# Row maxima of a 16,384 x 1,024 matrix: other blocks and loads, four half-row pieces at the end, and a written order of VectorE's steps

## The chip, the core and the metric

The kernel runs on one core of a Trainium2 chip. The metric is the time of one execution on the device in microseconds (us); lower is better. The profile is one such execution, seen by the hardware profiler.

## What is computed

```python
def setup_inputs():
    batch, seq, dim = 32, 512, 1024
    return {"x": np.random.randn(batch, seq, dim).astype(np.float32)}

def reference(x):
    return np.max(x, axis=-1).astype(np.float32)
```

The input is 16,384 rows of 1,024 float32 numbers, 67.1 MB. The output is the largest number of each row, 64 KB. Each number is read once and compared once, so the kernel is a stream of loads with a reduction behind it.

## The kernel before

**Layout.** The rows are cut into two blocks, of 112 and 16 + 2 = 18 rows for each of the 128 partitions. In a block, a partition owns consecutive rows of the input, so a load of n rows brings n x 4,096 consecutive bytes to each partition. `BLOCKS` lists the rows of the 17 loads; the last two rows of each partition come in three pieces. The loads land in `ring`, an SBUF buffer of 46 rows a partition, and the results gather in `res`, one column for each of a partition's 128 rows.

**VectorE** reduces each load to one number a row with `reduce_max` along the row (the helper `maximum`, L168). Each such reduction of load j is called here the direct reduction, `d`j.

**TensorE, ScalarE and GpSimd** take over a part. `SHARED` says of five loads how many of their last rows (m) are shared, and how many of the eight 128-column parts of such a row (parts) do not go to VectorE. A 128 x 128 part is called a block of a shared row; there are 38. For them `turn` (L125) transposes up to eight blocks with TensorE into PSUM (`ps`), ScalarE copies them to SBUF (`sb`), and GpSimd takes the maximum over the partitions with one `partition_all_reduce` (`top`, L143). `back` (L154) moves the results, one row of 128 numbers a block, back across the partitions with TensorE, into a small PSUM tile of the load (`fetched`, handed out by `share`). VectorE writes the maximum of the columns that it kept into a further column of the same tile (the partial reduction, `p`j), and `merge` (L170) reduces the tile's columns into `res` (`m`j). `MERGE` says after which load's steps a merge stands.

**Order.** Every computing engine works in the order in which the program emits its instructions (`in_turn` chains them). The loop over the loads emits VectorE's steps in the order of the loads, and TensorE's by the list `TENSOR`. Loads are issued on SyncE's queue, up to three ahead in the program's order, each as soon as the steps that still read its place in the ring are emitted; on the chip an issue then waits for these steps to be done.

**The end.** The row before last and the last row come as pieces of 689, 671 and 688 elements: the second holds the end of one row and the start of the next, and VectorE reduces both halves of it in one instruction (`res<-res 128x2`). The results of the first part of a row are put beside the elements that follow, so that the next reduction takes them in. Three stores of the first block's results, issued by ScalarE, wait for the first piece's reduction (`latest_row`), so that they run behind the loads; the second block's results are stored last.

Of the kernel before, what the change touches and what calls it, by code (L numbers as in the profile page):

```python
# [8 lines left out]
F32 = mybir.dt.float32  # L9
# [1 line left out]


BLOCKS = [
    [15, 15, 15, 14, 12, 11, 9, 8, 7, 6],
    [4, 3, 2, 2, 1, 1, 1],
]
RING = 46


SHARED = {7: (2, 3), 9: (4, 4), 11: (3, 3), 13: (2, 3), 16: (1, 1)}  # L20


TENSOR = [
    ("turn", 7, 0), ("back", 7, 0), ("turn", 9, 0), ("turn", 9, 1),
    ("back", 9, 0), ("turn", 11, 0), ("turn", 11, 1), ("back", 9, 1),
    ("turn", 13, 0), ("back", 11, 0), ("back", 11, 1), ("turn", 16, 0),
    ("back", 13, 0), ("back", 16, 0),
]

MERGE = {8: (7,), 12: (9,), 15: (11,), 18: (13, 16)}  # L30
NOSYNC = mybir.DependencyInfo(mybir.DependencyClass.NoSync, mybir.DependencyReason.DATA)
SYNC = mybir.DependencyInfo(mybir.DependencyClass.Sync, mybir.DependencyReason.DATA)


@with_exitstack
def kernel(
    ctx: ExitStack,
    tc: tile.TileContext,
    x: bass.AP,
    out: bass.AP,  # L40
):
    nc = tc.nc
    P = 128
    X = mybir.AxisListType.X
    ALU = mybir.AluOpType

    xf = x.flatten_outer_dims()
    N, D = xf.shape
    H = D // 2
    C = D // P  # L50
    I = N // P
    of = out.flatten_outer_dims()

    once = ctx.enter_context(tc.tile_pool(name="once", bufs=1))
    turned = ctx.enter_context(tc.tile_pool(name="turned", bufs=2))
    allr = ctx.enter_context(tc.tile_pool(name="allr", bufs=2))
    psum = ctx.enter_context(tc.tile_pool(name="psum", bufs=2, space=bass.MemoryType.PSUM))
    psmall = ctx.enter_context(tc.tile_pool(name="psmall", bufs=4, space=bass.MemoryType.PSUM))
    ring = once.tile([P, RING, D], F32)

    W = 336
    K = W - 1
    AT = I + 16
    MID = AT + K + W + 17
    res = once.tile([P, MID + D - W], F32)

    latest = {}

    def in_turn(engine, inst):

        if engine in latest:
            tc.add_manual_dep(inst.ins, latest[engine].ins.name, NOSYNC, reason="in turn")
        latest[engine] = inst
        return inst

    ident = once.tile([P, P], F32)  # L80
    colno = once.tile([P, P], F32)
    rowno = once.tile([P, 32], F32)
    in_turn("DVE", nc.vector.memset(ident, 1.0))  # L83
    in_turn("DVE", nc.vector.memset(rowno, 0.0))  # L84
    in_turn("DVE", nc.vector.tensor_tensor_scan(  # L85
        out=colno, data0=ident, data1=ident, initial=-1.0, op0=ALU.add, op1=ALU.mult))
    in_turn("DVE", nc.vector.transpose(out=rowno, in_=colno[:, :32]))  # L87
    for q in range(1, P // 32):
        part = rowno[q * 32:(q + 1) * 32, 0:1]
        in_turn("DVE", nc.vector.tensor_scalar(  # L90
            out=part, in0=part, scalar1=float(q * 32), scalar2=None, op0=ALU.add))
    in_turn("DVE", nc.vector.tensor_scalar(  # L92
        out=ident, in0=colno, scalar1=rowno[:, 0:1], scalar2=None, op0=ALU.is_equal))

    loads = []
    first = at = 0
    views = []
    for sizes in BLOCKS:
        S = sum(sizes) + 2 * (sizes is BLOCKS[-1])
        xb = xf[first * P:(first + S) * P, :].rearrange("(p i) d -> p i d", p=P)  # L100
        dst = bass.AP(tensor=of.tensor, offset=of.offset + first * P, ap=[[S, P], [1, S]])
        views.append((dst, res[:, first:first + S]))
        b = 0
        for n in sizes:
            if at + n > RING:
                at = 0
            loads.append((at, n, xb[:, b:b + n, :], first + b))
            at += n
            b += n
        first += S  # L110
    assert first == I

    def chunks(j):
        m, parts = SHARED[j]
        per = max(1, C // parts)
        return [(r, min(per, m - r)) for r in range(0, m, per)]

    def rows(j):
        start, n, _, _ = loads[j]
        return ring[:, start:start + n, :]  # L120

    tops = {}
    backs = {}

    def turn(j, c):  # L125


        m, parts = SHARED[j]
        r, q = chunks(j)[c]
        W = q * parts * P  # L130
        ps = psum.tile([P, D], F32)
        for i in range(q):
            for c0 in range(parts):
                k = i * parts + c0
                in_turn("PE", nc.tensor.transpose(  # L135
                    out=ps[:, k * P:(k + 1) * P],
                    in_=rows(j)[:, loads[j][1] - m + r + i, c0 * P:(c0 + 1) * P],
                    identity=ident,
                ))
        sb = turned.tile([P, D], F32)  # L140
        in_turn("ACT", nc.scalar.copy(out=sb[:, :W], in_=ps[:, :W]))  # L141
        top = allr.tile([P, D], F32)
        in_turn("POOL", nc.gpsimd.partition_all_reduce(  # L143
            top[:, :W], sb[:, :W], P, bass_isa.ReduceOp.max))
        tops[j, c] = top

    def share(j):
        m, parts = SHARED[j]
        if j not in backs:
            fetched = psmall.tile([P, parts + (parts < C), m], F32)  # L150
            backs[j] = fetched
        return backs[j]

    def back(j, c):  # L154

        m, parts = SHARED[j]
        r, q = chunks(j)[c]
        for i in range(q):
            for c0 in range(parts):
                k = i * parts + c0  # L160
                in_turn("PE", nc.tensor.transpose(  # L161
                    out=share(j)[:, c0, r + i:r + i + 1],
                    in_=tops[j, c][0:1, k * P:(k + 1) * P],
                    identity=ident[0:1, 0:1],
                ))

    def maximum(out, in_):
        return in_turn("DVE", nc.vector.reduce_max(out=out, in_=in_, axis=X))  # L168

    def merge(j):  # L170
        for i in MERGE.get(j, ()):
            _, k, _, c0 = loads[i]
            q, _ = SHARED[i]
            maximum(res[:, c0 + k - q:c0 + k], share(i).rearrange("p k m -> p m k"))


    issued = done = 0
    todo = list(TENSOR)
    for j in range(len(loads)):
        while issued < len(loads) and issued < j + 3:  # L180
            start, n, src, _ = loads[issued]
            held = any(s < start + n and start < s + k for s, k, _, _ in loads[j:issued])
            if held:
                break
            nc.sync.dma_start(out=rows(issued), in_=src)
            issued += 1
        while todo and todo[0][1] < (j if todo[0][0] == "back" else issued):
            what, i, c = todo.pop(0)
            (turn if what == "turn" else back)(i, c)
        _, n, _, col = loads[j]  # L190
        m, parts = SHARED.get(j, (0, 0))
        if n > m:
            maximum(res[:, col:col + n - m], rows(j)[:, :n - m, :])
        if m and parts < C:
            maximum(share(j)[:, parts, :], rows(j)[:, n - m:, parts * P:])
        merge(j)
    for what, i, c in todo:
        assert what == "back"
        back(i, c)

    if at + 1 > RING:
        at = 0
    piece = ring[:, at, :D - K]
    nc.sync.dma_start(out=piece, in_=xb[:, S - 2, :D - K])
    pair = xb[:, S - 2:, :].rearrange("p i d -> p (i d)")
    nc.sync.dma_start(out=res[:, AT:AT + K + W], in_=pair[:, D - K:D + W])
    nc.sync.dma_start(out=res[:, MID:], in_=pair[:, D + W:])
    latest_row = maximum(res[:, AT - 1:AT], piece)
    merge(len(loads))


    maximum(
        bass.AP(tensor=res.tensor, offset=res.offset + I - 2,
                ap=[list(res.ap[0]), [MID - 1 - (I - 2), 2]]),
        res[:, AT - 1:AT + K + W].rearrange("p (r k) -> p r k", r=2))
    merge(len(loads) + 1)
    maximum(res[:, I - 1:I], res[:, MID - 1:])


    for p, q in ((0, 48), (48, 96), (96, P)):  # L220
        store = nc.scalar.dma_start(out=views[0][0][p:q], in_=views[0][1][p:q])
        tc.add_manual_dep(store.ins, latest_row.ins.name, SYNC, reason="behind the loads")
    nc.scalar.dma_start(out=views[1][0], in_=views[1][1])


# [1 line left out]
_INS = ['x']  # L227
# [26 lines left out]
```

## Time and profile before

| | |
|---|---|
| time, median of 3 runs | 164.12 us (164.04 to 164.16) |
| span in the profile | 162.3 us |
| VectorE busy | 135.4 us |
| TensorE, ScalarE, GpSimd busy | 14.0, 6.3, 16.2 us |
| loads | 67.11 MB on queue q1 |

In the profile, DVE is VectorE, PE is TensorE's matrix multiplication, PEld its load of weights, ACT is ScalarE and POOL is GpSimd. A digit of a slice is the busy share of one fortieth of the span, in tenths. In a row of a group stand the line and engine, what is written from what, the shapes, then the busy time and the mean of one instruction, and after the second bar how long the engine was idle before it and what ended that. In a timeline, a row begins with the start and the duration in us; a bracket gives the idle time before it. A transpose of TensorE shows as MATMUL.

### The profile page before, as it was taken

Reading aid. Unit: us, or ns where it says so; the run is one execution under the profiler, and the core shown is the slowest. Engines: PE = TensorE matmul, PEld = TensorE weight load, DVE = VectorE, ACT = ScalarE, POOL = GpSimd, SP = SyncE. Lnnn points to the kernel's source line nnn. Section 1 sums busy time; section 2 is a strip of 40 time slices with the busy share of each in tenths; the row PEclk is TensorE's granted clock in tenths of the full one; section 3 lists DMA queues with packets and bytes.
Section 4 is the critical chain, followed back from the end, with each engine's and each line's share of the span. In section 5 each row is a group of like instructions: output and inputs, shape, how many; then the busy total and the mean of one; then the engine's idle time right before and its main releaser. Section 6 shows DMA issues by size and latency. Waiting matters only on the chain.

```text
span 162.3 us, 305 instructions
## 1 busy us (share of the span) xinstructions
PE 14.0 (9%) x76; PEld 12.0 (7%) x76; DVE 135.4 (83%) x35; ACT 6.3 (4%) x8; POOL 16.2 (10%) x11
## 2 busy tenths in 40 slices
PE   0000000000000000000000000000003010736540
PEld 0000000000000000000000000000002010725440
DVE  3000079995999779998999999999999999999994
ACT  3000000000000000000000000000001000222020
POOL 0000000000000000000000000000000500095970
DMA  7999699988999699999998998999999999999990
GB/s 242 485 485 454 273 485 485 485 379 348 485 485 485 285 410 452 452 452 388 497 472 371 433 455 355 436 436 420 509 396 445 452 395 396 440 411 423 405 379 18
DMA packets 3200, 67.18 MB, mean 414 GB/s; under 512 B 640, under 2 KB 640, under 8 KB 1408
## 3 DMA queue, kind: packets, MB, share of 16 engines
q1 hardware_dynamic: 2880, 67.11, 96.7%
q10 hardware_dynamic: 320, 0.07, 0.2%
HBM read 67.11 MB, written 0.07 MB: 414 GB/s over the span
## 4 chain that ended last, share of the span: by engine, by line
DVE 57%; DMA 36%; issue 5%; DVEq 0%
DVE res L168 52%; DMA ring<-in_x_dram 36%; DVE fetched L168 5%; DVEq L249 0%
## 5 line engine op out<-in xcount | busy, mean ns | idle before, releaser
L168 DVE TENSOR_REDUCE res<-ring 128x15 f32<-128x15360 f32 (+10 forms) x15 | 124.1, 8302 | 23.7 <-DMA ring<-in_x_dram 23.7
L143 POOL PARTITION_ALL_REDUCE top<-sb x7 | 16.0, 2330 | 141.8 <-ACT sb L141 141.8
L135 PE MATMUL ps<-ident,ring 128*128 128x128 f32 x38 | 9.3, 425 | 133.8 <-DMA ring<-in_x_dram 133.8
L135 PEld LDWEIGHTS ps<-ident,ring 128*128 128x128 f32 x38 | 7.5, 223 | 134.1 <-issue 127.8
L141 ACT COPY sb<-ps 128x768 f32<-128x768 f32 (+3 forms) x7 | 5.1, 739 | 150.2 <-PE ps L135 150.2
L168 DVE TENSOR_REDUCE fetched<-ring 128x2 f32<-128x1280 f32 (+3 forms) x5 | 8.5, 1699 | 0.0
L161 PE MATMUL fetched<-ident,top 1*128 1x1 f32 x38 | 4.8, 243 | 10.8 <-DVE fetched L168 7.3
L161 PEld LDWEIGHTS fetched<-ident,top 1*128 1x128 f32 x38 | 4.5, 213 | 12.5 <-issue 8.0
L168 DVE TENSOR_REDUCE res<-res 128x2 f32<-128x672 f32 (+1 forms) x2 | 1.7, 858 | 0.0
L141 ACT ACT_TABLE_LOAD x1 | 1.3, 1283 | 0.7 <-PEq L238 0.7
L83 DVE MEMSET ident<- 128x128 f32 x1 | 0.2, 165 | 0.8 <-PEq L238 0.8
L168 DVE TENSOR_REDUCE res<-fetched 128x2 f32<-128x8 f32 (+3 forms) x5 | 0.7, 158 | 0.0
L90 DVE TENSOR_SCALAR rowno<-rowno 32x1 f32<-32x1 f32 x3 | 0.4, 146 | 0.1
L85 DVE TENSOR_TENSOR_SCAN colno<-ident 128x128 f32<-128x128 f32 x1 | 0.4, 425 | 0.0
L92 DVE TENSOR_SCALAR ident<-colno,rowno 128x128 f32<-128x128 f32 x1 | 0.3, 285 | 0.0
L87 DVE STREAM_TRANSPOSE rowno<-colno 128x32 f32<-128x32 f32 x1 | 0.2, 213 | 0.0
L238 POOL MEMSET const-float32-0.0<- 128x1 f32 x1 | 0.1, 98 | 0.2 <-issue 0.2
L238 POOL MEMSET const-bfloat16-1.0<- 128x1 bf16 x1 | 0.1, 101 | 0.0
L238 POOL MEMSET const-uint8-127<- 128x1 uint8 x1 | 0.1, 101 | 0.0
L238 POOL MEMSET const-float32-1.0<- 128x1 f32 x1 | 0.1, 99 | 0.0
L84 DVE MEMSET rowno<- 128x32 f32 x1 | 0.1, 85 | 0.0
## 6 DMA issues: line engine op xcount, KB each, us to landing
ring<-in_x_dram SPq DMA_DIRECT2D x3, 7680.0 KB, 38.4
ring<-in_x_dram SPq DMA_DIRECT2D x1, 7168.0 KB, 37.0
ring<-in_x_dram SPq DMA_DIRECT2D x1, 6144.0 KB, 33.4
ring<-in_x_dram SPq DMA_DIRECT2D x1, 5632.0 KB, 28.6
ring<-in_x_dram SPq DMA_DIRECT2D x1, 4608.0 KB, 39.1
ring<-in_x_dram SPq DMA_DIRECT2D x1, 4096.0 KB, 33.3
ring<-in_x_dram SPq DMA_DIRECT2D x1, 3584.0 KB, 29.0
ring<-in_x_dram SPq DMA_DIRECT2D x1, 3072.0 KB, 35.9
```

The source lines that it names most:

```text
L83: in_turn("DVE", nc.vector.memset(ident, 1.0))
L84: in_turn("DVE", nc.vector.memset(rowno, 0.0))
L85: in_turn("DVE", nc.vector.tensor_tensor_scan(out=colno, data0=ident, data1=ident, initial=-1.0, op0=ALU.add, op1=ALU.mult))
L87: in_turn("DVE", nc.vector.transpose(out=rowno, in_=colno[:, :32]))
L90: in_turn("DVE", nc.vector.tensor_scalar(out=part, in0=part, scalar1=float(q * 32), scalar2=None, op0=ALU.add))
L92: in_turn("DVE", nc.vector.tensor_scalar(out=ident, in0=colno, scalar1=rowno[:, 0:1], scalar2=None, op0=ALU.is_equal))
L135: in_turn("PE", nc.tensor.transpose(out=ps[:, k * P:(k + 1) * P], in_=rows(j)[:, loads[j][1] - m + r + i, c0 * P:(c0 + 1) * P], identity=i ...
L141: in_turn("ACT", nc.scalar.copy(out=sb[:, :W], in_=ps[:, :W]))
L143: in_turn("POOL", nc.gpsimd.partition_all_reduce(top[:, :W], sb[:, :W], P, bass_isa.ReduceOp.max))
L161: in_turn("PE", nc.tensor.transpose(out=share(j)[:, c0, r + i:r + i + 1], in_=tops[j, c][0:1, k * P:(k + 1) * P], identity=ident[0:1, 0:1],))
L168: return in_turn("DVE", nc.vector.reduce_max(out=out, in_=in_, axis=X))
L238: nc = _bacc.Bacc("TRN2", target_bir_lowering=False, num_devices=1)
```

## The change

It gives the two blocks 96 and 32 rows a partition, and other loads: still 17, then four pieces instead of three, each a part of one row (424 + 600 and 572 + 452 elements). The number of blocks that go through TensorE stays 38, spread over six loads (12, 9, 9, 2, 4 and 2 blocks) instead of five (6, 16, 9, 6 and 1). `SHARED` lists them, and the turns and moves back are numbered in order (`t0` and `b0` are the first six blocks of load 9).

The order of the steps is written out in `PLAN`, for VectorE (`d`, `p`, `m`, and `f` for a piece) and TensorE (`t`, `b`) together, in the order in which their input is expected. A load is issued as soon as the steps that still read its place have been emitted, with no limit of three ahead. The ring has 47 rows, and `res` is now the front of the ring's tile. The early stores wait for the first piece's reduction, as before. What it is for: less idle time of VectorE at the start and the end, and a smaller step behind the last load.

```diff
 BLOCKS = [
-    [15, 15, 15, 14, 12, 11, 9, 8, 7, 6],
-    [4, 3, 2, 2, 1, 1, 1],
+    [16, 11, 14, 14, 12, 11, 10, 8],
+    [8, 7, 5, 3, 2, 2, 1, 1, 1],
 ]
-RING = 46
-SHARED = {7: (2, 3), 9: (4, 4), 11: (3, 3), 13: (2, 3), 16: (1, 1)}
-TENSOR = [
-    ("turn", 7, 0), ("back", 7, 0), ("turn", 9, 0), ("turn", 9, 1),
...
-MERGE = {8: (7,), 12: (9,), 15: (11,), 18: (13, 16)}
+RING = 47
+SHARED = {9: (2, 6), 10: (3, 3), 11: (3, 3), 13: (2, 1), 14: (1, 4), 16: (1, 2)}
+PIECES = [(424, 600), (572, 452)]
+PLAN = """
+    d0 d1 d2 d3 d4 d5 d6 d7 d8 t0 d9 t1 b0 p9 d10 t2 t3 p10 b1 t4 m9 p11 t5 b2 d12 b3 m10
+    p13 t6 b4 t7 p14 b5 d15 b6 m11 m13 p16 t8 f0 b7 f1 m14 f2 b8 f3 m16
+""".split()
...
-    ring = once.tile([P, RING, D], F32)
-    res = once.tile([P, MID + D - W], F32)
+    ring = once.tile([P, I + RING * D], F32)
+    res = ring[:, :I]
...
+    for r, widths in enumerate(PIECES):
+        c = 0
+        for q, w in enumerate(widths):
+            room = -(-(room + 1) // 16) * 16
+            pieces.append((ring[:, room:room + w], xb[:, S - last + r, c:c + w]))
+            if tail and q:
+                tail[-1] = (ring[:, room - 1:room], tail[-1][1])
+            tail.append((res[:, I - last + r:I - last + r + 1],
+                         ring[:, room - (q > 0):room + w]))
+            room += w
+            c += w
...
+            load = nc.sync.dma_start(out=rows(issued), in_=src)
             issued += 1
...
+    for step in PLAN:
+        issue()
+        kind, k = step[0], int(step[1:])
+        if kind in "dp":
+            (direct if kind == "d" else partial)(k)
+            readers[k] -= 1
+        elif kind == "t":
+            turn(k)
+            readers[chunks[k][0]] -= 1
+        elif kind == "b":
+            back(k)
+        elif kind == "m":
+            merge(k)
+        else:
+            inst = maximum(*tail[k])
+            if behind is None:
+                behind = inst
```

## The prediction

> **What bounds the kernel now.** I read the page's engine shares first, then its slices, its chain and its groups, then VectorE's timeline near the end.
>
> ```profile
> PE 14.0 (9%) x76; PEld 12.0 (7%) x76; DVE 135.4 (83%) x35; ACT 6.3 (4%) x8; POOL 16.2 (10%) x11
> DVE  3000079995999779998999999999999999999994
> DMA  7999699988999699999998998999999999999990
> q1 hardware_dynamic: 2880, 67.11, 96.7%
> DVE 57%; DMA 36%; issue 5%; DVEq 0%
> L168 DVE TENSOR_REDUCE res<-ring 128x15 f32<-128x15360 f32 (+10 forms) x15 | 124.1, 8302 | 23.7 <-DMA ring<-in_x_dram 23.7
> ```
>
> Two resources are full: the loads' queue keeps the 16 DMA engines busy for 96.7% of the span, and VectorE has no zero after the fifth slice. The last row says where VectorE's slack went: it waits 23.7 us, all for loads, and the slices put this in the first half. The chain agrees, since from 74.64 on it is practically VectorE alone. The timeline of VectorE's last part:
>
> ```profile
> 21.42 16.15 DVE L168 TENSOR_REDUCE res<-ring 128x15 f32<-128x15360 f32 x1 [18.91 <-DMA ring<-in_x_dram]
> 39.55 16.15 DVE L168 TENSOR_REDUCE res<-ring 128x15 f32<-128x15360 f32 x1 [1.98 <-DMA ring<-in_x_dram]
> 57.70 16.16 DVE L168 TENSOR_REDUCE res<-ring 128x15 f32<-128x15360 f32 x1 [1.99 <-DMA ring<-in_x_dram]
> 74.64 55.86 DVE L168 TENSOR_REDUCE res<-ring 128x14 f32<-128x14336 f32 x5 [0.79 <-DMA ring<-in_x_dram]
> ...
> 152.51 1.48 DVE L168 TENSOR_REDUCE fetched<-ring 128x2 f32<-128x1280 f32 x1
> 153.90 2.38 DVE L168 TENSOR_REDUCE res<-ring 128x1 f32<-128x1024 f32 x2
> 156.20 0.16 DVE L168 TENSOR_REDUCE res<-fetched 128x3 f32<-128x12 f32 x1
> 156.34 1.09 DVE L168 TENSOR_REDUCE fetched<-ring 128x1 f32<-128x896 f32 x1
> 157.34 0.86 DVE L168 TENSOR_REDUCE res<-ring 128x1 f32<-128x689 f32 x1
> 158.24 0.85 DVE L168 TENSOR_REDUCE res<-res 128x2 f32<-128x672 f32 x1
> 159.01 0.22 DVE L168 TENSOR_REDUCE res<-fetched 128x2 f32<-128x8 f32 x2
> 159.15 0.86 DVE L168 TENSOR_REDUCE res<-res 128x1 f32<-128x689 f32 x1
> ```
>
> Set these starts beside the trace's landing records: loads 14, 15 and 16 and the three pieces landed at 153.76, 155.04, 156.31, 157.22, 158.13 and 158.98. The steps on them start at 153.90, 155.06, 156.34, 157.34, 158.24 and 159.15. So VectorE reaches the tail with no backlog: transfer and reduction end together, and a change gains only if both get shorter at the end.
>
> **What the skill says.** "DMA: Bandwidth & Descriptors", section "Where 436 GB/s comes from", gives a ceiling of 435.2 GB/s for the 16 ports. The trace agrees: loads of 15 rows land 18.14 us apart and one of 14 rows 16.95, about 1.205 us for one row of 512 KB more, which is 435 GB/s. "VectorE: DVE Perf Modes", section "The perf-mode tier table", has the reduction at its plain rate only, one element in a cycle of 0.96 GHz. The trace agrees: 16,155 less 15,086 ns for 1,024 elements is 1.04 ns each. The same page, section "The DRAIN you can't avoid", says that an operation reading what the previous one on VectorE wrote needs a semaphore. Here queued reductions start some 0.08 us before their predecessor's end (153.90 before 153.99), while the one at 158.24 reads what the previous wrote and starts 0.04 after that one's end at 158.20.
>
> **The change part by part.**
>
> The stream of loads. Landing spacings fit 0.07 us a load plus 1.205 a row (single rows: 1.27 to 1.29). Both versions load 126 rows in 17 loads before the pieces, so load 16 lands where it does now, at about 156.3. The pieces: packets of 2,684 to 2,756 bytes took 115 ns each in the trace's packet records, 8 to an engine; packets of 8,192 took 313, so 0.0367 ns a byte and some 13 ns fixed. Pieces of 424, 600, 572 and 452 elements then take 0.61, 0.82, 0.78 and 0.64 us, and land at 156.9, 157.7, 158.5 and 159.1. The fourth piece costs the stream 0.1 us.
>
> The ring. Rings of 46 and 47 rows hold the queue full: in the new layout the load that waits longest for space is load 7, freed by the reduction of load 3 at about 84.9, while the stream is busy until load 6 lands at 109.8. I price the ring at nothing; the queued loads hide it. Where the results lie (inside the ring's tile now) adds no instruction and no wait in the built order of loads: nothing.
>
> VectorE's work. 38 blocks go through TensorE in both, so VectorE reads the same 1,024 x 128 - 38 x 128 elements (and two carried cells in both). The reductions go from 27 to 29: 13 direct, 6 partial, 6 merges, 4 of pieces. A queued reduction takes 1.067 us a row plus 0.06 from start to start (14 rows: 74.64 to 89.64; 2 rows: 139.41 to 141.60), a merge 0.08. The two more cost 0.06 + 0.08 = 0.14 us. Of the four pieces two pairs depend on each other directly (the second and the fourth read the cell that the step just before wrote); now one pair does. That adds 0.12.
>
> VectorE's idle time, by the same two rules, load by load. Load 0 lands at 22.6, 1.2 later than now. Load 1 is smaller (11 rows, at 35.9), and is there when load 0 is reduced at 39.8. The reduction of load 2 waits from 51.55 to 52.9 (1.3 us), that of load 3 from 67.9 to 69.8 (1.9), loads 4 and 5 do not wait, load 6 lands at 109.8 where VectorE is free at 109.5 (0.3), load 8 gives 0.1. These count from where the next could have started, 0.08 before the end; so counted, today's waits are 2.06 + 2.07 + 0.87 = 5.0. Sum: 1.2 more at the start, 3.65 in place of 5.0 later: 0.15 less idle, and 0.06 less where today's step at 156.34 waits for its landing.
>
> TensorE in front of VectorE. In the built order the partial of load 9 (128x2) waits for TensorE: `b0` stands before `p9` in the plan and both write one PSUM tile. Load 9 lands at 137.7. From the first turn of six blocks now: TensorE starts at 123.24, GpSimd ends at 125.68 + 2.50 = 128.18, so 4.94 us; then 0.05 and 0.77 for six moves back; start after landing 0.05 to 0.14. `b0` is done at 143.5 to 143.7. VectorE is free at 143.2 (137.8 plus 5 rows, 5.40). A stall of 0.3 to 0.45 us, I take 0.4; queued behind it is all the rest of VectorE's work. All of it is lost: without it `p9` would end at 143.8, just when load 10 lands.
>
> The other chains of PE, ACT and POOL have slack: with copies of 0.27 to 0.80 us and GpSimd at 1.50 (three blocks) and 2.50 (six), about 0.35 a block plus 0.42, the last (load 16, two blocks) is brought back at about 159.0, before the merge that needs it.
>
> The tail. After `p9`, VectorE has no wait left: `d10` starts at 144.2 (landed 143.8), `p11` 148.5 (147.5), `d12` 150.6 (150.0), `p13` 152.9 (152.5), `p14` 154.8 (153.7), `d15` 155.4 (155.0), `p16` 156.65 (156.3), the pieces 157.5 (156.9), 158.15 (157.7), 158.9 (158.5) and 159.7 (159.1). The last piece is shorter (453 elements, 0.53 in place of 0.78), but it starts 0.5 late, and `m16` follows with 0.08. The end is 160.37. The same addition for the order of now gives 159.93 where the trace has 160.01, so I read 160.45, 0.44 later than now. As terms: 0.14 for two more reductions, 0.12 for the dependent pair, 0.4 for `b0`, less 0.15 and 0.06 of idle time, 0.45. The store behind it now carries 32 results a partition and not 16: 0.02 by the packet times of 64 and 448 bytes (11 and 25 ns). Sum: 0.46, so 164.12 + 0.46 = 164.58, say 164.6.
>
> What is between: the early stores, now behind the first piece's step, are released at about 158.1, as now (158.23); today their first packet runs at 159.12 and the last load packet ends at 158.53, so they do not meet. Nothing for them.
>
> **The rivals.**
>
> Backlog gone by the end, so that the transfer sets it. For it: VectorE gains 0.138 us on each row against the stream, and my waits of 0.3, 0.1 and 0.4 each hang on differences of two large sums. Then the last piece (159.12) is reduced at about 159.2 + 0.61, the merge ends at 159.9, some 0.1 before 160.01: 164.0. Half of the backlog gone gives 164.3. Not slower by the bound.
>
> The loads get slower. A load of 16 rows is 65,536 bytes a partition, larger than any in the trace (61,440); were each packet split, 8 x 13 ns = 0.1 us come to the first landing and pass to the end. The last 32 rows now step 128 KB from partition to partition, not 72 KB; no trace shows that stride. A bound from both sides: nothing, or 2% of the last 38 us of stream, 0.8. Against it: the packets show one rate at all sizes. 164.7 to 165.4.
>
> Faster by more than 0.2%. This needs an end 0.33 earlier, 159.7, so the last piece landed by 159.0 and no backlog: four pieces for nothing and smaller last step in full. The packet times speak against it. 163.75.
>
> **How the numbers follow.** 0.56 for the backlog of 0.25 to 0.8 us at the end (164.35 to 164.9), 0.24 for it mostly gone (164.0 to 164.35), 0.12 for slower loads, 0.08 for faster. The bound of 0.2% is 0.33 us, so slower begins at 164.45: most of the first case and all of the third, 0.64; same 0.28. The range, 164.0 to 165.0, leaves out the faster case and the far end of slower loads.
>
> **What would show it.** Right: loads landing every 1.205 us a row to the end; VectorE waiting on TensorE near 143.3 and on loads at about 51.6, 67.9 and 109.5; no wait after 144; the last piece's reduction starting about 0.5 us after landing, the last merge ending near 160.45. Wrong: `p9` starting at once; a step on a piece starting within 0.1 us of its landing; row spacing over 1.21 us in the last loads; a span at or under 162.0.

## The result, and the profile after

The changed kernel took 164.53 us (median of 5 runs, 164.17 to 164.60), the kernel before 164.04 us (163.95 to 164.16) beside it: ratio 1.0026, 95% interval 1.0013 to 1.0038. A second set of runs on another occasion gave 1.0039 (1.0025 to 1.0054). So it is slower, by 0.3 to 0.4%; the forecast was 164.6 us, 0.46 us more than before.

From the page of the changed kernel, the engines' shares, two rows of slices, the loads' queue, the chain by engine and the costliest group:

```profile
PE 14.6 (9%) x76; PEld 12.0 (7%) x76; DVE 135.6 (83%) x37; ACT 6.7 (4%) x10; POOL 16.9 (10%) x13
DVE  3000049999996999689999999999999999999994
DMA  7989989999999999898898999799989899999990
q1 hardware_dynamic: 3024, 67.11, 96.5%
DMA 56%; DVE 35%; issue 3%; POOL 2%; PE 1%; ACT 0%; SPq 0%; DVEq 0%
L73 DVE TENSOR_REDUCE ring<-ring 128x11 f32<-128x11264 f32 (+12 forms) x17 | 125.8, 7427 | 23.4 <-DMA ring<-in_x_dram 23.3
```

By the shares, the slices, the queue and the last row nothing has changed: VectorE is as busy as before and waits as long for loads, and the queue is as full. What differs stands in the chain by engine, where POOL, PE and ACT now have shares. They had none. (That DMA and DVE have changed places says less. The chain gives DMA the whole time from the issue of load 9 at 98.06 to its landing, and most of it load 9 spent behind other loads: load 8 landed at 129.11.) The chain in order of time (start, duration, what) shows where they enter:

```profile
98.06 39.55 DMA ring<-in_x_dram
137.61 0.09 issue
137.70 1.53 PE ps L137 x6
139.23 0.02 issue
139.25 0.81 ACT sb L143
140.06 0.08 issue
140.15 2.52 POOL top L145
142.66 0.04 issue
142.70 0.81 PE got L155 x6
143.51 0.02 issue
143.54 0.69 DVE got L73
```

Load 9 lands at 137.61, goes through TensorE, ScalarE, GpSimd and TensorE again, and only then does VectorE start `p9`. VectorE's own timeline has the wait, and the end:

```profile
129.13 14.08 DVE L73 TENSOR_REDUCE ring<-ring 128x8 f32<-128x8192 f32 x2
143.54 0.69 DVE L73 TENSOR_REDUCE got<-ring 128x2 f32<-128x512 f32 x1 [0.32 <-PE got L155]
...
156.59 0.95 DVE L73 TENSOR_REDUCE got<-ring 128x1 f32<-128x768 f32 x1
157.45 1.40 DVE L73 TENSOR_REDUCE ring<-ring 128x1 f32<-128x424 f32 x2
158.76 0.15 DVE L73 TENSOR_REDUCE ring<-got 128x1 f32<-128x5 f32 x1
158.83 1.40 DVE L73 TENSOR_REDUCE ring<-ring 128x1 f32<-128x572 f32 x2
160.15 0.15 DVE L73 TENSOR_REDUCE ring<-got 128x1 f32<-128x3 f32 x1
```

After the 0.32 us no row has a bracket: VectorE waits for nothing any more but its own previous step, 0.03 us at each of the two steps that read what the step just before wrote (inside the rows at 157.45 and 158.83). By the landing records load 16 lands at 156.24 and its step starts at 156.59, 0.35 late; in the kernel before the same step started 0.03 after the landing. That backlog reaches the end. The last step ends at 160.30, in the kernel before at 160.01.

The end of VectorE's last step less the landing of load 16 separates VectorE's part from shifts of the whole stream, and is used below as "the distance": 3.70 us before (160.01 - 156.31), 4.06 after (160.30 - 156.24). Each distance is that of one profiled execution. It leaves out what follows VectorE's last step, the store and the end of the program: 2.30 us before, 2.35 after.

### The profile page after: what moved, and what is told of

Same layout as the page of the kernel before. It is cut to its first block, busy times and chain, and to the rows that moved or that the text cites. A ratio compares the mean times of both kernels' runs of the same rounds, so it can differ in the third digit from the quotient of the medians.

```text
span 162.7 us, 321 instructions
## 1 busy us (share of the span) xinstructions
PE 14.6 (9%) x76; PEld 12.0 (7%) x76; DVE 135.6 (83%) x37; ACT 6.7 (4%) x10; POOL 16.9 (10%) x13
## 4 chain that ended last, share of the span: by engine, by line
DMA 56%; DVE 35%; issue 3%; POOL 2%; PE 1%; ACT 0%; SPq 0%; DVEq 0%
DMA ring<-in_x_dram 56%; DVE ring L73 31%; DVE got L73 4%; POOL top L145 2%; PE ps L137 1%; PE got L155 0%; ACT sb L143 0%; SPq L210 0%; DVEq L264 0%
## 5 line engine op out<-in xcount | busy, mean ns | idle before, releaser
L73 DVE TENSOR_REDUCE ring<-ring 128x11 f32<-128x11264 f32 (+12 forms) x17 | 125.8, 7427 | 23.4 <-DMA ring<-in_x_dram 23.3
L145 POOL PARTITION_ALL_REDUCE top<-sb x9 | 16.7, 1898 | 141.5 <-ACT sb L143 141.1
L73 DVE TENSOR_REDUCE got<-ring 128x3 f32<-128x1920 f32 (+4 forms) x6 | 8.5, 1441 | 0.3 <-PE got L155 0.3
L155 PE MATMUL got<-ident,top 1*128 1x1 f32 x38 | 5.3, 245 | 3.5 <-POOL top L145 3.5
L155 PEld LDWEIGHTS got<-ident,top 1*128 1x128 f32 x38 | 4.7, 209 | 5.8 <-POOL top L145 4.8
L73 DVE TENSOR_REDUCE ring<-got 128x3 f32<-128x12 f32 (+4 forms) x6 | 0.8, 156 | 0.0
```

The source lines that it names most:

```text
L145: in_turn("POOL", nc.gpsimd.partition_all_reduce(top[:, :W], sb[:, :W], P, bass_isa.ReduceOp.max))
L155: in_turn("PE", nc.tensor.transpose(out=share(j)[:, c, r + i:r + i + 1], in_=tops[k][0:1, w:w + P], identity=ident[0:1, 0:1],))
```

## The experiments

My theory (A): VectorE's queue sets the end, and the wait of `p9` for `b0` makes most of the loss, with the four pieces as a smaller part. Rivals: the wait is a plain term that goes when the two are swapped (B); the wait costs nothing, because landings set the steps after it (C); the pieces are the loss (D); a gain from the pieces hides a larger loss from the new layout of the loads (E).

**The swap** (`e1_swap`): `p9` ahead of `b0`.

```diff
-    ... d9 t1 b0 p9 d10 t2 t3 p10 b1 ...
+    ... d9 t1 p9 b0 d10 t2 t3 p10 b1 ...
```

> The changed kernel with p9 ahead of b0 in the plan, so that VectorE no longer waits for TensorE there. In the changed kernel VectorE waits 0.32 us at 143.2 and its last merge ends at 160.30. Theory A (the wait is one of VectorE's, but b0 now waits for p9 in TensorE's queue and t2 stands behind it): p9 starts at 143.2, the turn of load 10 and with it GpSimd's chain begin about 0.7 later, m13 then waits about 0.3 for b6, and the last merge ends at 160.2 to 160.3, no better. Rival B (the wait is a plain term of the sum): no new wait, last merge at 159.95, 0.3 earlier. Rival C (the wait cost nothing, landings set the steps after it): d10 to p16 start as in the changed kernel, within 0.1.

Measured: ratio 1.0028 (1.0016 to 1.0039), distance 4.05, no better. (The clock time of the last merge, 160.54, is over the 160.2 to 160.3 expected, as load 16 landed later here, at 156.49.) VectorE's timeline of the swapped order:

```profile
143.38 0.68 DVE L73 TENSOR_REDUCE got<-ring 128x2 f32<-128x512 f32 x1
143.99 2.29 DVE L73 TENSOR_REDUCE ring<-ring 128x2 f32<-128x2048 f32 x1
...
156.36 0.16 DVE L73 TENSOR_REDUCE ring<-got 128x3 f32<-128x12 f32 x1
156.75 0.16 DVE L73 TENSOR_REDUCE ring<-got 128x2 f32<-128x4 f32 x1 [0.23 <-PE got L155]
156.83 0.95 DVE L73 TENSOR_REDUCE got<-ring 128x1 f32<-128x768 f32 x1
```

`p9` starts without a wait, and `m13` waits for TensorE 13 us later. TensorE's row of `b0` and GpSimd's timeline have the way between. `b0` in the swapped order:

```profile
144.21 0.77 PE L155 MATMUL got<-ident,top 1*128 1x1 f32 x6 [3.46 <-DVE got L73]
```

GpSimd first in the changed kernel, then in the swapped order:

```profile
140.15 4.99 POOL L145 PARTITION_ALL_REDUCE top<-sb  x2 [139.72 <-ACT sb L143]
146.35 3.91 POOL L145 PARTITION_ALL_REDUCE top<-sb  x2 [1.22 <-ACT sb L143]
```

```profile
140.40 4.99 POOL L145 PARTITION_ALL_REDUCE top<-sb  x2 [139.98 <-ACT sb L143]
147.44 8.85 POOL L145 PARTITION_ALL_REDUCE top<-sb  x5 [2.05 <-ACT sb L143]
```

`b0` now waits for `p9`, the turn of load 10 stands behind `b0` on TensorE, so GpSimd's next reductions start at 147.44 and not at 146.35, and five of them then run back to back up to `b6`, which `m13` needs. The wait had moved. B falls. C explains the time too, but by C `d10` would start where it did. It starts 0.02 us after the landing of load 10 (143.99, 143.97) and in the changed kernel 0.43 after it (144.14, 143.71): the backlog was gone there, and the wait of `m13` brought it back.

**The turn first** (`e2_turn_first`, and once more as `e10_turn_first_again`): `p9` ahead of `b0`, but the turn of load 10 ahead of `b0` too.

```diff
-    ... t1 b0 p9 d10 t2 t3 p10 b1 ...
+    ... t1 p9 t2 b0 d10 t3 p10 b1 ...
```

> The changed kernel with the order p9 t2 b0 d10 t3 p10: p9 doesn't wait for b0, and the turn of load 10 doesn't stand behind b0. Theory A: p9 starts at 143.2, the turn of load 10 at its landing (143.8), GpSimd's chain as in the changed kernel, no wait at m13; the last merge ends 0.3 to 0.4 earlier, at 159.9 to 160.0, which is the end of the kernel before (160.01): ratio to before 0.999 to 1.000. Rival B: the same. Rival C: 160.2 to 160.3.

> The turn-first order once more on the same chip, for a profile without late landings: last merge 3.70 to 3.78 us behind the landing of load 16, ratio 1.0000 to 1.0010.

Measured: 1.0006 (0.9998 to 1.0015), and 1.0009 (1.0003 to 1.0016) the second time. The distance is 3.74 both times, 0.32 less than in the changed kernel, the very length of the wait. The first profile is of the longest execution of its set (164.77 us, median 164.13), in which load 16 landed at 156.90, so the clock time forecast for the last merge is missed there (160.64); in the second it is 160.10, against 159.9 to 160.0 expected. From the timeline of the second:

```profile
143.25 0.68 DVE L73 TENSOR_REDUCE got<-ring 128x2 f32<-128x512 f32 x1
143.86 2.29 DVE L73 TENSOR_REDUCE ring<-ring 128x2 f32<-128x2048 f32 x1
...
156.38 0.96 DVE L73 TENSOR_REDUCE got<-ring 128x1 f32<-128x768 f32 x1
157.25 1.40 DVE L73 TENSOR_REDUCE ring<-ring 128x1 f32<-128x424 f32 x2
158.57 0.15 DVE L73 TENSOR_REDUCE ring<-got 128x1 f32<-128x5 f32 x1
158.64 1.40 DVE L73 TENSOR_REDUCE ring<-ring 128x1 f32<-128x572 f32 x2
159.95 0.15 DVE L73 TENSOR_REDUCE ring<-got 128x1 f32<-128x3 f32 x1
```

Load 10 lands at 143.84 and `d10` starts at 143.86; load 16 lands at 156.36 and `p16` starts at 156.38. The backlog is gone.

**A longer wait** (`e3_two_waits`): `b1` ahead of `p9` as well.

```diff
-    ... t1 b0 p9 d10 t2 t3 p10 b1 ...
+    ... t1 b0 b1 p9 d10 t2 t3 p10 ...
```

> The changed kernel with b1 also ahead of p9, so that VectorE waits for both moves back. Theory A: p9 starts at 146.0 to 146.6 instead of 143.54, some 2.5 to 3 later, and the whole of it arrives at the end: last merge at 162.8, ratio to before 1.017 to 1.02. Rival C (landings set the steps near the end and swallow a wait in the middle): last merge under 161.

Measured: 1.0183 (1.0169 to 1.0197), distance 6.51, last merge at 162.96. The row of `p9`, and the last:

```profile
146.19 0.69 DVE L73 TENSOR_REDUCE got<-ring 128x2 f32<-128x512 f32 x1 [2.81 <-PE got L155]
...
162.81 0.15 DVE L73 TENSOR_REDUCE ring<-got 128x1 f32<-128x3 f32 x1
```

The wait is 2.81 - 0.32 = 2.49 us longer, the distance 6.51 - 4.06 = 2.45. With the turn-first order this is the same finding from both sides: a wait of VectorE at 143 us arrives at the end nearly whole. C falls.

**The pieces alone** (`e4_old_loads`): the new code with the blocks, loads, shared rows and order of the kernel before, but the four pieces. (The second of these blocks has 14 + 2 = 16 rows a partition, not the 18 given further up and in the expectation.)

```diff
-    [16, 11, 14, 14, 12, 11, 10, 8],
-    [8, 7, 5, 3, 2, 2, 1, 1, 1],
+    [15, 15, 15, 14, 12, 11, 9, 8, 7, 6],
+    [4, 3, 2, 2, 1, 1, 1],
-SHARED = {9: (2, 6), 10: (3, 3), 11: (3, 3), 13: (2, 1), 14: (1, 4), 16: (1, 2)}
+SHARED = {7: (2, 3), 9: (4, 4), 11: (3, 3), 13: (2, 3), 16: (1, 1)}
```

> The changed kernel's code with the blocks, the loads, the shared rows and the order of steps of the kernel before (112 and 18 rows, 15, 15, 15, 14 ... rows a load), and the four new pieces at the end; f2 f3 m16 stand last. Theory A (the end pieces cost VectorE one more reduction and one more step that directly reads what the one before wrote, less a smaller last step): last merge at 160.0 to 160.15, ratio to before 1.000 to 1.001. Rival D (the four pieces are the loss): last merge at 160.3, ratio 1.002 to 1.003. Rival E (the pieces are a gain, the loads' layout a larger loss): last merge at 159.8, ratio 0.998 to 0.999.

Measured: 1.0010 (1.0004 to 1.0017), distance 3.88, last merge at 160.19, just over the 160.15 expected. That is a quarter to 0.4 of the loss in time and half of it in distance, where D wanted all of it, and of the wrong sign for E. The step of load 16 starts at 156.34 for a landing at 156.31, so nothing is late here but the end itself: 0.18 us more behind load 16 than the three pieces took.

**Merges between dependent steps**, on the new loads with the turn first (`e5_tail_order`, the end of its order below) and, in the same way, on the old loads (`e7_old_tail`: `p16 b6 f0 m11 f1 f2 m13 m16 f3`).

```diff
-    m11 m13 p16 t8 f0 b7 f1 m14 f2 b8 f3 m16
+    m11 p16 t8 f0 m13 b7 f1 f2 b8 m14 m16 f3
```

> The turn-first order (p9 t2 b0 d10 t3 p10) with merges put between the steps that read each other's output: m11 p16 f0 m13 f1 f2 m14 m16 f3 at the end. Theory A: each of the two direct reads costs about 0.12 because the reader must wait for the writer's end, and a merge between them fills that time; with m16 ahead of f3 the last step is f3. Last step 0.1 to 0.2 earlier than in the turn-first order alone, against its last load: ratio to before 0.9990 to 1.0000, a tie or a gain of at most 0.1%. Rival: only the sum of instructions counts, order at the end does nothing: 1.0006 as the turn-first order alone.

> The old loads with the four pieces, with merges between the steps that read each other's output: p16 f0 m11 f1 f2 m13 m16 f3. Theory A: 0.1 to 0.15 earlier than the old loads with the pieces' steps one behind the other (1.0010): ratio 1.0000 to 1.0004. Rival (order at the end does nothing): 1.0010.

Measured: 1.0012 (1.0005 to 1.0020) and 1.0009 (1.0001 to 1.0017). Neither came out as I expected. The distances say why on the first: 3.69 against 3.74, so 0.05 was won and not 0.1 to 0.2. `f1` and `f3` lose their gaps, as meant, but `p16` has a new one behind `m11`:

```profile
156.46 0.16 DVE L73 TENSOR_REDUCE ring<-got 128x3 f32<-128x12 f32 x1
156.69 0.96 DVE L73 TENSOR_REDUCE got<-ring 128x1 f32<-128x768 f32 x1
```

It starts 0.09 us after the landing of load 16 (156.59), where it started 0.02 after it in the turn-first order. It doesn't read what `m11` writes, and in the kernel before and in `e4_old_loads`, where `m11` stands directly ahead of it as well, it starts 0.02 after the landing too. The trace's records show another difference: here `p16` has two waits, one for its load and one for an earlier step of VectorE itself, and so it has in two of the orders below (`e6_swap_late`, `e9_three_pieces`), where it starts 0.09 late as well. In all other runs it has only the first. These three are the orders on the new loads with `m13` behind `p16`. A likely reading from the program: the small PSUM tiles take turns in four buffers, the tile of load 16 takes that of load 10, so `p16` must follow `m10`, and `m13`, while it stood in front, had made a separate wait for that unnecessary. No run tests it.

On the old loads the distance falls by 0.14, from 3.88 to 3.74, as expected, but the median time by only 0.05 us (164.21 to 164.16). Part of the rest stands behind VectorE's last step: from there to the end of the span it is 2.28 us in `e4_old_loads` and 2.34 here, as SyncE, which at the end waits for all that is still open, has one wait more to go through after the last store has landed. (On the new loads likewise: 2.34 with the turn first, 2.41 with this end.) What is left the times do not resolve.

**The swap with a late merge** (`e6_swap_late`): the swapped order with `m13` behind `f1`.

```diff
-    b6 m11 m13 p16 t8 f0 b7 f1 m14 f2
+    b6 m11 p16 t8 f0 b7 f1 m13 m14 f2
```

> The swapped order (p9 b0) with m13 moved from before p16 to behind f1. Theory A: in the swapped order the wait only went from p9 to m13, since GpSimd's chain is 1.1 later; with m13 behind f1 its input is there in time, VectorE has no wait at 156.5, and the last merge ends about 0.2 earlier against its last load than in the swapped order: ratio to before 1.001 to 1.0015. Rival (the loss in the swapped order has another cause than m13's wait): ratio stays at 1.0028.

Measured: 1.0028 (1.0017 to 1.0040), not the 1.001 to 1.0015 expected; the distance is 4.00, so only 0.05 was won. The wait at `m13` is gone, but the timeline shows what came instead:

```profile
156.32 0.16 DVE L73 TENSOR_REDUCE ring<-got 128x3 f32<-128x12 f32 x1
156.55 0.96 DVE L73 TENSOR_REDUCE got<-ring 128x1 f32<-128x768 f32 x1
157.42 1.40 DVE L73 TENSOR_REDUCE ring<-ring 128x1 f32<-128x424 f32 x2
158.74 0.34 DVE L73 TENSOR_REDUCE ring<-got 128x2 f32<-128x4 f32 x2
```

`p16` starts 0.09 us after the landing of load 16 (156.46), against 0.34 in the swapped order: 0.25 won. But `m13` now stands behind the landing, and the two merges take 0.34 us where two back to back take 0.23 (the row at 156.23 or 156.44 in the other orders): `m14` waits for `b7`, since GpSimd's chain is still late. From the start of `p16` to that of `f2` it is 0.20 us longer than in the swapped order (2.44 against 2.24). The late merge cannot pay for a late GpSimd.

**The changed kernel again** (`e8_after_again`).

> The changed kernel once more, beside these three on one chip: last merge 1.4 to 1.5 us behind the landing of the last piece, ratio 1.002 to 1.003.

Measured: 1.0039 (1.0025 to 1.0054), over the 1.002 to 1.003 expected; distance 4.06 and the wait 0.32, both the same to 0.01. Its last merge ends 1.48 behind the last piece (160.31 - 158.83), as expected.

**The best of both** (`e9_three_pieces`): new loads, turn first, the old three pieces.

```diff
+    pieces = [
+        (ring[:, AT - D:AT - D + 689], pair[:, :689]),
+        (ring[:, AT:AT + 671], pair[:, 689:1360]),
+        (ring[:, MID:MID + 688], pair[:, 1360:]),
+    ]
...
-    ... m11 m13 p16 t8 f0 b7 f1 m14 f2 b8 f3 m16
+    ... m11 p16 t8 f0 m13 b7 f1 m14 f2 b8 m16
```

> The new loads in the turn-first order, with the end of the kernel before: pieces of 689, 671 and 688 elements, the middle one reduced as two halves in one step, in the order p16 f0 m13 f1 m14 f2 m16. Theory A: the effects add up, 1.0006 of the turn-first order less the 0.0010 that the four pieces cost on the old loads, so 0.9994 to 1.0000; the last step ends 3.5 to 3.65 us behind the landing of load 16 (3.70 in the kernel before, 3.74 in the turn-first order). Rival (VectorE is at its landings by then, so nothing is left to win): ratio 1.0003 to 1.0008, 3.7 or more.

Measured: 164.04 us against 164.05 beside it, 1.0004 (0.9995 to 1.0012), distance 3.69. With the turn first, which had won most of it back, this repairs the change (about 0.3%), but it does not beat the kernel before. The distance is not the 3.5 to 3.65 of A, and both figures lie at the rival's, though the interval of the time holds A's range as well. In its timeline the step of load 16 starts at 156.29, 0.10 after the landing at 156.19, and each piece within 0.2 us of its own. The 0.10 is the late `p16` of the two orders above. So VectorE is near its landings here, but not at them, and an order without that delay was not run.

## Why the prediction was right, point by point

**The bound, right.** Transfer and reduction end together before; VectorE's queue decides after. The longer wait (2.45 us of distance for 2.49) and the turn-first order (0.32 for 0.32) show it.

**The wait of `p9` for `b0`, right.** Forecast 0.3 to 0.45 at 143.2, taken 0.4; it is 0.32 at 143.21. That the whole of it is lost was argued, and is now measured: 0.32 of the distance.

**The reductions and the dependent pair, right in kind.** A step that stands directly behind the one whose output it reads starts 0.03 to 0.04 us after that one's end in every trace, where others with their input there start about 0.08 before it. The pieces on the old loads cost 0.18 of distance. On the new loads 0.13 of that is returned by the shorter `p16` (768 elements and not 896), which I had only inside the sum of all elements. So the distance is 3.70 + 0.32 + 0.18 - 0.13 = 4.07, where 4.06 was measured; the 0.13 is worked out from the 128 elements and has no run of its own.

**Idle time at the start, right in size and of no worth.** First landing 22.48 (forecast 22.6), later waits 1.25, 1.86, 0.23 and 0.02. Counted as in the forecast, from 0.08 before the previous end, they are 1.33, 1.94, 0.32 and 0.10, forecast 1.3, 1.9, 0.3 and 0.1; start included 0.24 less than before, where I had 0.15. But VectorE without the `b0` wait stands at its landings again by load 10, as in the kernel before. From there the landings set its steps and earlier idle time no longer counts. My sum of terms took 0.15 off the end for it; it should have begun anew at load 10. It also left out the 0.13 of the shorter `p16`. The two nearly cancel, so that the sum of terms (0.45) met the addition step by step (0.44) by luck.

**The stream, mis-sized.** The fourth piece was priced at 0.1 us with a last landing at 159.1. It is 158.85: from load 16 to the last piece 2.61 us, with three pieces 2.67 before and 2.56 in `e9_three_pieces`, so a fourth piece cost the stream 0.05 at most. Packets of 1,696, 1,808, 2,288 and 2,400 bytes took 71, 75, 93 and 101 ns where I had 76, 80, 98 and 102. It did no harm to the sum, as VectorE was late by more: the last piece's step starts at 159.61, 0.76 after the landing, and not about 0.5. The rival of slower loads did not come: packets of 65,536 bytes took 2,419 ns, in line with the others, and the last single rows land 1.28 to 1.29 apart as before. (The stride of the old second block, given as 72 KB, is 64 KB: 16 rows of 4 KB.)

**The rest.** Ring, stores and the place of the results show no cost, as said: load 16 lands no later than before (156.24, before 156.31), and the early stores are released at 158.06 (158.23 before), and their first packet runs at 158.95, after the last load's at 158.41.

**The size, right in part by luck.** The last merge was forecast at 160.45 and ends at 160.30. Of the 0.15 too much, 0.08 is the correction that I added because the same addition came out 0.08 short for the kernel before, and the rest is mostly the wait, taken at 0.4 (`d10` starts at 144.14, forecast 144.2). In the profile the span is 0.34 us longer than before: 0.36 of distance and 0.05 behind VectorE's last step (0.02 was forecast), less 0.07 for an earlier load 16. The medians are 0.49 and, in the second set, 0.52 us longer. The profiled execution is shorter than the median of its set (164.43, 164.53), and the last section has what may make others longer; it is not in the prediction. So the time, forecast 0.46 longer, fits better than the steps do.

## What to carry to other kernels

Where two engines exchange results through queues that run in order, a wait is removed only if the work behind the released instruction does not move as well: look at what stands behind it in both queues before swapping. Price a wait by whether its engine later runs up against something else, a landing for instance: before that point idle time is forgotten; after it, here, every part of a microsecond arrived at the end. A smaller last piece was no gain here, since it bought one more step that directly depends on the one before it (0.18 us of distance). And after a change of order look at all steps behind it: a merge moved away left another step with a second wait and 0.07 us later.

## What the runs showed of the hardware

A load lands in sixteen parts, one of each DMA engine, and the parts of the first and the last engine lie apart. In the changed kernel the distance stays at 0.45 to 0.50 us from the first load (21.98 and 22.48) to the last piece. In the execution with the latest landings (the first of the turn-first order) it is 0.78 at the first load (21.95 and 22.73) and grows to 1.1 by load 5, where it stays. So in the nine profiles of the new loads the first engine's part of load 16 lands at 155.8 to 156.0, but the last engine's, which the steps wait for, at 156.19, 156.24, 156.25, 156.36, 156.45, 156.46, 156.49, 156.59 and once 156.90. In the three profiles of the old loads it lands at 156.30 to 156.31. VectorE passes such a lag on, with a backlog or without: the distance is 3.74 for 156.36 and for 156.90, and 4.05 to 4.06 for 156.24 and for 156.49. If the other executions of the new loads land like these profiles, in the middle 0.14 us later than the old ones, that is a part of their time that no order of VectorE's steps wins back, and it may be why the turn-first order, with nearly the old distance, still took 0.1 to 0.2 us longer; no run tested it.
